# Block 0's weighted sums of gathered expert rows: from VectorE to 32-column TensorE matmuls, two tokens a step

## The chip, the core and the metric

The kernel runs on one core of a Trainium2 chip. The metric is the device time of one execution in microseconds (us), as the median of several runs. A core has a matmul engine (TensorE, PE in the rows; its weight loads are PEld), a vector engine (VectorE, DVE), an activation engine (ScalarE, ACT), a general engine (GpSimd, POOL) and a sync engine that issues DMA transfers (SyncE, SP); the DMA engines move the data. Each engine executes its own instruction stream in order; semaphores tie the streams together.

## The reference, cut to what matters

The program is one decoder layer for 1024 tokens of width 1024: a first norm, one wide projection, two kinds of attention, gates, an output projection, an attention over 256 memory tokens, and last an expert mixer (PEER) of 16,384 experts. The change touches the mixer only:

```
q  = (h @ w_q).reshape(n, 8, 2, 64)                 # 8 heads, two halves
sc = einsum('nhcd,hckd->nhck', q, sub_keys)         # 128 keys in each half
s_top, i_top = top_k(sc, 16)                        # 16 best keys in each half
cand_s = s_top[:, :, 0, :, None] + s_top[:, :, 1, None, :]
cand_i = i_top[:, :, 0, :, None] * 128 + i_top[:, :, 1, None, :]
best_s, pos = top_k(cand_s, 16)                     # 16 best pairs in each head
g = softmax(best_s); idx = cand_i at pos            # 8 x 16 = 128 slots a token
a = einsum('cd,ced->ce', h, u[idx])                 # h . u of each slot's expert
a = gelu(a) * g
out = einsum('ce,ced->cd', a, v[idx])               # weighted sum of 128 rows of v
```

## The kernel before

The 1024 tokens are eight blocks of 128. Everything up to the mixer runs in two token groups of four blocks: projections (P), attentions (T), branch and gate products (G), output projection (O), memory attention (M), expert queries (R). `queries` of the first group are ready when the second group begins, and the mixer of its four blocks (0 to 3) is laid beside the second group's stages.

The mixer is computed in two ways. For blocks 0 to 3 the rows of `u` and `v` are *gathered*: for each of a token's 128 slots one indirect DMA on GpSimd brings 128 rows (one per token, 512 KB) into one of seven row buffers (`R_BUFS`). `gathered_u` multiplies a row by `h3` and sums along it (VectorE, L1039); `gathered_v` adds weight times row to a running sum (L1058). The lane "experts" runs U and V of the blocks in the order of `ORDER`. For blocks 4 to 7 the mixer is *dense*: all 128 groups of 128 experts are multiplied for all 512 tokens, `uT` against `fT` and the result, weighted by a matrix `c`, against `v`. The weights matrix `Wd` is built from the selected slots by `weights` and passes through DRAM. Of the 128 groups (called experts in what follows) the first 48 (`EARLY`) have their `u` product computed first, while `weights` still runs: each one's gelu goes to DRAM (`ga`) and comes back later as `c`. Then all 128 run in turn with two accumulators, `kept` and `out`.

Matmuls of the dense part are three-pass: an operand is split into a high part (ScalarE, L106) and a remainder (VectorE, L107), and `mm3` issues three matmuls (L129 to L131). For the second group's projections, branch and memory products the operands are whole float32 instead (one matmul, L127). The gate products of a group are deferred: `fill` issues them (128 matmuls, four column blocks) beside other work. Transposes go through TensorE into PSUM tiles of the name `tps`, two buffers (`tps()`), from which each consumer copies out. In the second group this holds for keys (L371), queries (L355), attention rows.

Routing (`route`, with `top16` at L928 to L932) finds the top 16 per half and the top 16 pairs, on VectorE, one yield after another; for blocks 0 to 3 in the lane "routes", for 4 to 7 within `weights`.

The order of the work: the program's code emits a main line of stages; at its steps `Pace.tick(us)` gives each lane a budget, and a lane emits its next piece when its price (`U_EACH`, `ROUTE_EACH`) is covered. A scheduler then places every instruction by data dependences and priority; a lane's pieces carry a lag (`ROUTE_LAG`, `EXPERT_LAG`), which puts them behind the main line where both could go. `issue_after` ties an instruction behind another on the same engine. The order within each engine is fixed when the program is built.

## Time and profile before

| | before |
|---|---|
| median of 3 runs | 3502.35 us |
| lowest, highest | 3493.39, 3512.26 us |
| the profiled execution | 3509.34 us |
| its span in the profile | 3507.6 us |
| mean granted TensorE clock in it | 0.928 |

The span is what the instruction records cover; the time of an execution includes a little around it. Busy time of an engine is the sum over its records; matmuls overlap, so TensorE's busy time is above what their starts take. [...] In order of time, the second group's projections take 660 to 1004 us, its attentions end at 1287, branch to queries at 1638; the first 48 experts go to 2119, the first `kept` matmul is at 2240, and the last one ends at 3470.6.

### The profile page before, as it was taken

The numbers are of one execution on the slowest core, as the hardware profiler recorded it, in microseconds if no ns is written. First come the engines' busy times: TensorE is split into PE (matmuls) and PEld (weight loads), VectorE is DVE, ScalarE is ACT, GpSimd is POOL, SyncE is SP. The second block draws the span as 40 slices with busy tenths as digits, with TensorE's granted clock in tenths as the row PEclk, the third lists the DMA queues.
The fourth block names the chain that finished last, engine by engine and source line by source line (L and its number), as shares of the span: only waits on it lengthen the run. The fifth ranks groups of instructions, "written<-read, shape, count | busy, mean of one in ns | idle before, by whom it ended". The sixth has DMA issues, their size and how long they took to land.

```text
span 3507.6 us, 42342 instructions
## 1 busy us (share of the span) xinstructions
PE 3015.4 (86%) x13234; PEld 2285.7 (65%) x13234; DVE 2878.4 (82%) x6695; ACT 1396.7 (40%) x2537; POOL 1380.4 (39%) x1122
## 2 busy tenths in 40 slices
PE   8999888798787698686989995588899999999995
PEld 7777766553355575455767774466687788777884
DVE  6656544599888879888988988687799999999998
ACT  5755344245565441322546456222222222222221
POOL 0000000011235246553131466333466665767665
PEclk9999998999898799888999998799899999999998
DMA  4575443436789579897485899999999999999997
GB/s 138 162 186 133 162 140 137 132 121 198 223 259 312 139 272 356 306 328 272 163 314 189 309 379 341 375 309 321 318 351 372 376 380 365 382 379 373 383 382 265
DMA packets 394210, 964.65 MB, mean 275 GB/s; under 512 B 36712, under 2 KB 146048, under 8 KB 392576
## 3 DMA queue, kind: packets, MB, share of 16 engines
q0 software_dynamic: 155264, 560.01, 45.0%
q1 hardware_dynamic: 238720, 401.94, 33.3%
q8 instruction: 104, 1.70, 0.2%
q14 instruction: 122, 1.00, 0.1%
HBM read 871.64 MB, written 90.18 MB: 274 GB/s over the span
## 4 chain that ended last, share of the span: by engine, by line
PE 35%; DVE 21%; DMA 17%; issue 15%; POOL 8%; ACT 4%; SPq 1%; POOLq 0%; ACTq 0%; DVEq 0%
POOL rows L1036 5%; PE acc L129 5%; PE acc L131 5%; PE acc L130 5%; DMA c<-ga 4%; DVE h3s L1058 3%; DMA rows<-in_peer_v_dram,ii 2%; DMA so<-pq 2%; PE fill L127 2%; POOL rows L1052 2%; PE po L720 2%; DVE rows L1039 2%; DMA fraw<-in_w_in_dram 1%; DMA rows<-in_peer_u_dram,ii 1%; PE tps L601 1%
## 5 line engine op out<-in xcount | busy, mean ns | idle before, releaser
L1036 POOL DMA_INDIRECT rows<-in_peer_u_dram,ii x512 | 656.8, 1283 | 917.2 <-DVE rows L1039 304.9
L1052 POOL DMA_INDIRECT rows<-in_peer_v_dram,ii x512 | 660.6, 1290 | 447.4 <-DVE h3s L1058 290.9
L1058 DVE SCALAR_TENSOR_TENSOR h3s<-rows,wexp,h3s 128x1024 f32<-128x1024 f32 x508 | 651.1, 1282 | 34.4 <-DMA rows<-in_peer_v_dram,ii 25.1
L1039 DVE SCALAR_TENSOR_TENSOR rows<-rows,h3s 128x1024 f32<-128x1024 f32 x512 | 612.0, 1220 | 62.7 <-DMA rows<-in_peer_u_dram,ii 62.2
L129 PE MATMUL acc<-fT,uT 128*128 128x512 f32 x1024 | 415.6, 406 | 38.6 <-ACT uT L106 23.2
L131 PE MATMUL acc<-fT,uT 128*128 128x512 f32 x1024 | 411.8, 402 | 15.3 <-DVE uT L107 15.2
L130 PE MATMUL acc<-fT,uT 128*128 128x512 f32 x1024 | 410.5, 401 | 0.0
L106 ACT ACTIVATE c<-wl 128x512 fp32r<-128x512 f32 x128 | 80.2, 631 | 805.6 <-PE out L130 479.2
L143 POOL TENSOR_TENSOR rstd<-msq,mhalf 128x1 f32<-128x1 f32 (+1 forms) x42 | 34.0, 808 | 596.1 <-DVE msq L141 572.5
L129 PEld LDWEIGHTS acc<-fT,uT 128*128 128x128 f32 x1024 | 196.5, 192 | 84.7 <-ACT uT L106 23.6
L131 PEld LDWEIGHTS acc<-fT,uT 128*128 128x128 f32 x1024 | 196.7, 192 | 64.4 <-DVE uT L107 23.7
L106 ACT ACTIVATE uT<-uraw 128x1024 fp32r<-128x1024 f32 x128 | 135.6, 1059 | 254.2 <-PE acc L130 131.0
L130 PE MATMUL kept<-v,c 128*128 128x512 f32 x512 | 206.2, 405 | 32.3 <-DVE v L107 32.2
L129 PE MATMUL kept<-v,c 128*128 128x512 f32 x512 | 201.4, 400 | 37.1 <-ACT v L106 35.8
L130 PEld LDWEIGHTS acc<-fT,uT 128*128 128x128 f32 x1024 | 197.0, 192 | 45.3 <-issue 6.0
L129 PE MATMUL out<-v,c 128*128 128x512 f32 x512 | 203.6, 398 | 15.2 <-DVE accu L1282 15.2
L107 DVE TENSOR_TENSOR w<-wraw,w 128x512 fp32r<-128x512 f32 (+1 forms) x176 | 116.4, 680 | 116.3 <-ACT w L106 109.5
L131 PE MATMUL kept<-v,c 128*128 128x512 f32 x512 | 203.7, 398 | 0.0
L130 PE MATMUL out<-v,c 128*128 128x512 f32 x512 | 201.9, 394 | 0.0
L131 PE MATMUL out<-v,c 128*128 128x512 f32 x512 | 201.8, 394 | 0.0
L562 ACT ACTIVATE junk<-W,xb 128x384 bf16<-128x384 f32 (+5 forms) x186 | 163.7, 880 | 78.8 <-DVE xb L560 76.1
L127 PE MATMUL acc<-wraw,hT 128*128 128x512 f32 (+1 forms) x384 | 169.3, 597 | 16.2 <-ACT tok L349 7.6
(367 smaller groups left out, 6731.6 us busy)
## 6 DMA issues: line engine op xcount, KB each, us to landing
uraw<-in_peer_ut_dram SPq DMA_DIRECT2D x128, 512.0 KB, 9.2
vraw<-in_peer_v_dram SPq DMA_DIRECT2D x128, 512.0 KB, 8.8
Wd<-wbuf SPq DMA_DIRECT2D x64, 512.0 KB, 8.6
wl<-Wd SPq DMA_DIRECT2D x64, 512.0 KB, 8.4
wraw<-in_w_in_dram SPq DMA_DIRECT2D x40, 512.0 KB, 3.6
fraw<-in_w_in_dram SPq DMA_DIRECT2D x32, 512.0 KB, 6.0
wraw<-in_w_out_dram SPq DMA_DIRECT2D x24, 512.0 KB, 4.2
ga<-gelu SPq DMA_DIRECT2D x48, 256.0 KB, 5.4
```

What stands on the lines that cost most here:

```text
L106: self.nc.scalar.activation(hi, src, AF.Copy)
L107: self.last_dve = self.nc.vector.tensor_tensor(lo, src, hi.bitcast(F32), op=OP.subtract).ins
L127: self.last_pe = nc.tensor.matmul(out, l[0], r[0], start=start, stop=stop).ins
L129: nc.tensor.matmul(out, l[0], r[0], start=start, stop=False)
L130: nc.tensor.matmul(out, l[0], r[1], start=False, stop=False)
L131: self.last_pe = nc.tensor.matmul(out, l[1], r[0], start=False, stop=stop).ins
L562: nc.scalar.activation(junk[:, :(b + 1) * P], self.W[b], AF.Sign, bias=xb[:, j:j + 1].bitcast(F32), accum_out=s[:, j:j + 1])
L720: nc.tensor.matmul(po[:, h * 64:(h + 1) * 64], pT[:, j * P:(j + 1) * P], self.dsv[:, k0 + j, gg * 64:(gg + 1) * 64], start=(k0 + j == 0), ...
L1036: nc.gpsimd.indirect_dma_start(out=u, out_offset=None, in_=a["peer_u"][0], in_offset=bass.IndirectOffsetOnAxis(ap=ii[:, j:j + 1], axis=0))
L1039: nc.vector.scalar_tensor_tensor(u, u, 1.0, h3, op0=OP.mult, op1=OP.mult, accum_out=aa[:, j:j + 1])
L1052: nc.gpsimd.indirect_dma_start(out=v, out_offset=None, in_=a["peer_v"][0], in_offset=bass.IndirectOffsetOnAxis(ap=r["ii"][:, j:j + 1], axi ...
L1058: nc.vector.scalar_tensor_tensor(o, v, w[:, j:j + 1], o, op0=OP.mult, op1=OP.add)
```

## The change

Block 0's V leaves the lane "experts" (`ORDER`), and a lane of its own, "tiled", does it (`tiled_v`). `slots` transposes block 0's slot ids on TensorE (through `tps()`) to `iiT`, where a column holds one token's 128 slots. In each of 64 steps two gathers fetch the 128 rows of `v` of two tokens, and four matmuls of 32 columns contract over the 128 slots: two tokens by two halves of the 1024 columns, each into its own 32 partitions of one PSUM bank (`vacc`). The stationary operand `z` is a 128 x 32 tile of zeros in which the token's own column holds its weights; the 32 tokens of a tile accumulate one after another. A finished PSUM tile goes through ScalarE and DRAM to the block's sum. A step waits for both gathers (`add_manual_dep`) and is tied behind the last emitted matmul; matmuls that `mm3` emits afterwards are tied behind the step (`behind`). The lane starts once the last attention stage has given back its PSUM and block 0's U products are emitted, and it is drained at the end of the first 48 experts. The PSUM bank comes from the stages that follow: five accumulators in G to R for six, three in the first 48 experts for four. SBUF comes from `gelu` and `gT`, one buffer each for two. The price of a gathered item in the last stage is 2.4 for 2.0.

```diff
@@ -80,6 +81,8 @@
     def __init__(self, tc, a, out, dbg=None):
         self.tc, self.nc, self.a, self.out, self.dbg = tc, tc.nc, a, out, dbg
         self.pace = Pace(tc)
+        self.vps = self.pe_gate = None
+        self.multiplied = set()
@@ -121,12 +124,18 @@
+    def behind(self, start=True):
+        return self.tc.issue_after(self.pe_gate) if start and self.pe_gate is not None else nullcontext()
     def mm3(self, out, l, r, start, stop):
         nc = self.nc
         if len(l) == 1:
-            self.last_pe = nc.tensor.matmul(out, l[0], r[0], start=start, stop=stop).ins
+            with self.behind(start):
+                self.last_pe = nc.tensor.matmul(out, l[0], r[0], start=start, stop=stop).ins
             return
-        nc.tensor.matmul(out, l[0], r[0], start=start, stop=False)
+        with self.behind(start):
+            nc.tensor.matmul(out, l[0], r[0], start=start, stop=False)
         nc.tensor.matmul(out, l[0], r[1], start=False, stop=False)
         self.last_pe = nc.tensor.matmul(out, l[1], r[0], start=False, stop=stop).ins
@@ -1023,6 +1032,12 @@
         nc.vector.tensor_copy(r["gg"], r["g"].rearrange("p h s -> p (h s)"))
         r["ii"] = ep.tile([P, P], I32, name="ii", bufs=NG)
         nc.vector.tensor_copy(r["ii"], ids)
+        if b in TILED:
+            t = self.tps()
+            nc.tensor.transpose(t[:, :P], ids, self.ident)
+            r["iiT"] = ep.tile([P, P], I32, name="iiT", bufs=len(TILED))
+            nc.vector.tensor_copy(r["iiT"], t[:, :P])
         yield
@@ -1038,6 +1053,71 @@
             with self.tc.issue_after(self.last_dve):
                 nc.vector.scalar_tensor_tensor(u, u, 1.0, h3, op0=OP.mult, op1=OP.mult, accum_out=aa[:, j:j + 1])
             yield self.u_each
+        self.multiplied.add(b)
+    def tiled_v(self, blks):
+        nc, a, ep = self.nc, self.a, self.ep
+        for b in blks:
+            while self.vps is None or b not in self.multiplied:
+                yield 5.0
+            r = self.rs[b]
+            w = ep.tile([P, P], F32, name="wexp", bufs=1)
+            nc.scalar.activation(w, r["aa"], AF.Gelu)
+            nc.vector.tensor_tensor(w, w, r["gg"], op=OP.mult)
+            o = self.vps.tile([P, 512], F32, name="vacc", bufs=1)
+            nc.tensor.transpose(o[:, :P], w, self.ident)
+            wT = r["gg"].rearrange("p (h s t) -> p h s t", h=2, s=2)
+            nc.scalar.activation(r["gg"], o[:, :P], AF.Copy)
+            done = self.scratch([P, D], f"vo{b}")
+            def gather(n):
+                vs = []
+                for s in range(2):
+                    at = n // 32 * 64 + 32 * s + n % 32
+                    v = self.rows()
+                    i = nc.gpsimd.indirect_dma_start(out=v, out_offset=None, in_=a["peer_v"][0],
+                                                     in_offset=bass.IndirectOffsetOnAxis(ap=r["iiT"][:, at:at + 1], axis=0))
+                    vs.append((v, i.ins))
+                return vs
+            nx = gather(0)
+            for n in range(64):
+                h, t = divmod(n, 32)
+                if t == 0:
+                    o = self.vps.tile([P, 512], F32, name="vacc", bufs=1)
+                if t % 4 == 0:
+                    z = ep.tile([P, 2, 128], F32, name="z", bufs=2)
+                    nc.gpsimd.memset(z, 0.0)
+                    nc.vector.tensor_copy(z[:, :, t:t + 33 * 3 + 1:33], wT[:, h, :, t:t + 4])
+                vs, nx = nx, gather(n + 1) if n < 63 else None
+                with self.tc.high_priority(offset=EXPERT_LAG), self.tc.issue_after(self.last_pe):
+                    m = None
+                    for s in range(2):
+                        for c in range(2):
+                            q = 32 * (2 * s + c)
+                            i = nc.tensor.matmul(o[q:q + 32], z[:, s, 32 * (t % 4):32 * (t % 4) + 32],
+                                                 vs[s][0][:, c * 512:(c + 1) * 512], start=t == 0, stop=t == 31).ins
+                            if m is None:
+                                self.tc.add_manual_dep(i, vs[1][1].name, SYNC, reason="the tokens go together")
+                            m = i
+                self.last_pe = self.pe_gate = m
+                yield self.v_each
+                if t == 31:
+                    e = self.rows()
+                    nc.scalar.activation(e[:, :512], o, AF.Copy)
+                    for s in range(2):
+                        for c in range(2):
+                            q, at = 32 * (2 * s + c), 64 * h + 32 * s
+                            nc.sync.dma_start(done[at:at + 32, c * 512:(c + 1) * 512], e[q:q + 32, :512])
+            self.pe_gate = None
+            o = self.rows()
+            nc.sync.dma_start(o, done)
+            self.finish(b, o, [self.rows() for _ in range(3)])
+            yield 1.0
     def gathered_v(self, b, r):
@@ -1133,7 +1213,7 @@
             nc.tensor.transpose(t[:, P:2 * P], r["g"].rearrange("p h s -> p (h s)"), self.ident)
             ni = wb.tile([P, P], I32, name="ni")
             nc.vector.tensor_copy(ni, t[:, :P])
-            gT = wb.tile([P, P], F32, name="gT", bufs=2)
+            gT = wb.tile([P, P], F32, name="gT", bufs=1)
             nc.scalar.activation(gT, t[:, P:2 * P], AF.Copy)
             yield 1.0
@@ -1188,7 +1268,7 @@
             stores.pop(0)()
             yield 3.0
-    def dense(self, psum, early):
+    def dense(self, psum, early, vpx):
         nc, a = self.nc, self.a
@@ -1221,11 +1301,13 @@
                 self.pace.add("weights", self.weights(blks))
                 for e in range(early):
                     o = first(e)
-                    t = self.wb.tile([P, 512], F32, name="gelu", bufs=2)
+                    t = self.wb.tile([P, 512], F32, name="gelu", bufs=1)
                     nc.scalar.activation(t, o, AF.Gelu)
                     ga[e] = self.scratch([P, 512], f"ga{e}")
                     nc.sync.dma_start(ga[e], t)
                 self.pace.drain("weights")
+                self.pace.drain("tiled")
+                vpx.close()
             self.route_ctx.close()
             psum = self.psum_phase(psum, "ps3", A_BUFS)
             kept = {}
@@ -1333,8 +1415,11 @@
-            psum = self.psum_phase(psum, f"psG{g}", 6)
             last = g == len(GROUPS) - 1
+            if last:
+                vpx = ExitStack()
+                self.vps = vpx.enter_context(self.pool("vps", side="right", space=PSUM))
+            psum = self.psum_phase(psum, f"psG{g}", 5 if last else 6)
@@ -1375,18 +1460,21 @@
                 self.u_each = U_EACH[0]
                 self.pace.add("routes", routes, ROUTE_EACH, ROUTE_LAG)
                 self.pace.add("experts", self.experts(routes), None, EXPERT_LAG)
+                self.v_each = V_TILED
+                self.pace.add("tiled", self.tiled_v(TILED), None, EXPERT_LAG)
         self.pace.drain("routes")
         psum = self.psum_phase(psum, "ps2", D_BUFS)
-        psum = self.dense(psum, EARLY)
+        psum = self.dense(psum, EARLY, vpx)
 EARLY = 48
 V_AHEAD, V_EACH = 0, None
-ORDER = [("U", 0), ("V", 0), ("U", 1), ("V", 1), ("U", 2), ("V", 2), ("U", 3), ("V", 3)]
+TILED, V_TILED = (0,), 6.0
+ORDER = [("U", 0), ("U", 1), ("V", 1), ("U", 2), ("V", 2), ("U", 3), ("V", 3)]
-H_BUFS, D_BUFS, R_BUFS = (4, 2), 4, 7
+H_BUFS, D_BUFS, R_BUFS = (4, 2), 3, 7
@@ -1394,7 +1482,7 @@
-U_EACH, ROUTE_EACH = (1.9, 1.8, 1.9, 1.3, 2.0), 3.0
+U_EACH, ROUTE_EACH = (1.9, 1.8, 1.9, 1.3, 2.4), 3.0
```

The order on TensorE at the end of the second group's projections, before: the gate products (`fill`), the projections (`acc<-wraw,hT`) and the transposes of keys (`k_...`) and queries (`tok`).

```order
L127 MATMUL fill<-hT_6126,fraw 128x512 x2
L127 MATMUL acc<-wraw,hT_6126 128x328 x8
L127 MATMUL fill<-hT_6126,fraw 128x512
L371 MATMUL tps<-ident,k_6655 128x128 x3
L127 MATMUL acc<-wraw,hT_6126 128x512
L371 MATMUL tps<-ident,k_6680 128x128 x2
L127 MATMUL acc<-wraw,hT_6126 128x512
```

The same place after, with the transpose of the slot ids (`ids`):

```order
L135 MATMUL fill<-hT_6126,fraw 128x512 x2
L135 MATMUL acc<-wraw,hT_6126 128x328 x8
L135 MATMUL fill<-hT_6126,fraw 128x512
L135 MATMUL acc<-wraw,hT_6126 128x512 x32
L135 MATMUL fill<-hT_6126,fraw 128x512 x125
L1038 MATMUL tps<-ident,ids 128x128
L380 MATMUL tps<-ident,k_6659 128x128 x3
L380 MATMUL tps<-ident,k_6684 128x128 x3
```

All 32 remaining projection matmuls and all 125 remaining gate products now stand in front of the first key transpose, and the transpose of the ids stands between.

The order on VectorE in the first of the dense experts, before: the remainder splits `uT` of experts 4 to 6 (the numbers are buffers) and routing instructions, the rows between them left out.

```order
L107 TENSOR_TENSOR uT_14007<-uraw,uT_14006 128x1024
L975 MAX key<-ci 128x8
...
L996 TENSOR_REDUCE ids<-eq 128x32
L107 TENSOR_TENSOR uT_14108<-uraw,uT_14107 128x1024
...
L932 MAX_INDEX i_15117<-v_15116,t_15120 128x8
L107 TENSOR_TENSOR uT_14176<-uraw,uT_14175 128x1024
```

The same place after, experts 4 to 8:

```order
L110 TENSOR_TENSOR uT_14369<-uraw,uT_14368 128x1024
...
L1251 SCALAR_TENSOR_TENSOR ah<-dot,gT 128x512
L110 TENSOR_TENSOR uT_14481<-uraw,uT_14480 128x1024
...
L110 TENSOR_TENSOR uT_14557<-uraw,uT_14556 128x1024
...
L1138 SCALAR_TENSOR_TENSOR h3s<-rows,wexp,h3s 128x1024
L110 TENSOR_TENSOR uT_14620<-uraw,uT_14619 128x1024
L1138 SCALAR_TENSOR_TENSOR h3s<-rows,wexp,h3s 128x1024 x2
L110 TENSOR_TENSOR uT_14733<-uraw,uT_14732 128x1024
```

Between the splits of experts 4 and 5 stood 20 VectorE instructions and now stand 291; 98 more come before that of expert 6 and 211 before that of expert 7, after which two stand before the next.

The order on TensorE in the branch products of the second group, before:

```order
L127 MATMUL acc<-oT_8649,wraw 128x512 x64
```

The same place after, with the matmuls of the steps (`vacc`):

```order
L135 MATMUL acc<-oT_8653,wraw 128x512 x13
L1101 MATMUL vacc<-rows,z 32x512
L135 MATMUL acc<-oT_8653,wraw 128x512 x2
L1101 MATMUL vacc<-rows,z 32x512
L135 MATMUL acc<-oT_8653,wraw 128x512
L1101 MATMUL vacc<-rows,z 32x512 x10
L135 MATMUL acc<-oT_8653,wraw 128x512 x10
```

The 64 branch matmuls, which stood together, have matmuls of steps between them, often one at a time. Over the whole program the 256 matmuls of the 64 steps stand in 119 runs, 73 of them of a single matmul and 36 of four; 38 steps lie in the stages G to R, 26 in the first 48 experts, the last of these before expert 33.

## Rows read from the trace of the kernel before

**Rows 1.** The page of the profile: busy time, share, instructions; one DMA group.
```profile
span 3507.6 us, 42342 instructions
...
PE 3015.4 (86%) x13234; PEld 2285.7 (65%) x13234; DVE 2878.4 (82%) x6695; ACT 1396.7 (40%) x2537; POOL 1380.4 (39%) x1122
...
ga<-gelu SPq DMA_DIRECT2D x48, 256.0 KB, 5.4
```
**Rows 2.** Windows by stage: us; busy PE, PEld, DVE, ACT, POOL; PEclk; DMA; GB/s.
```profile
728.00:1004.00 276.00, 225.57 (x641) 113.63 (x641) 243.38 (x1161) 164.16 (x329) 50.32 (x49) 0.91 0.60 189
...
1287.00:1638.00 351.00, 266.27 (x886) 173.67 (x886) 304.78 (x495) 81.11 (x157) 208.96 (x171) 0.84 0.90 334
...
1679.00:2013.00 334.00, 301.66 (x1533) 234.58 (x1532) 300.84 (x1131) 178.19 (x230) 94.32 (x73) 0.96 0.68 248
...
2119.00:2240.00 121.00, 65.19 (x384) 51.29 (x384) 97.54 (x110) 58.90 (x75) 74.04 (x58) 0.81 0.95 355
2240.00:2594.00 354.00, 303.74 (x1212) 239.68 (x1213) 285.97 (x386) 85.78 (x113) 142.52 (x115) 0.92 0.93 321
2594.00:3452.00 858.00, 839.42 (x3652) 687.56 (x3651) 821.05 (x991) 235.69 (x306) 568.36 (x424) 0.99 1.00 375
```
**Rows 3.** Timeline of PE in the last experts: start us, us, engine, line.
```profile
3439.72 0.39 PE L130 MATMUL out<-v,c 128*128 128x512 f32 x1
...
3441.08 0.39 PE L130 MATMUL out<-v,c 128*128 128x512 f32 x1
```
**Rows 4.** Instruction groups by line: count, busy us, mean ns, idle before and its releaser.
```profile
L1058 DVE SCALAR_TENSOR_TENSOR h3s<-rows,wexp,h3s 128x1024 f32<-128x1024 f32 x508 | 651.1, 1282 | 34.4 <-DMA rows<-in_peer_v_dram,ii 25.1
L1039 DVE SCALAR_TENSOR_TENSOR rows<-rows,h3s 128x1024 f32<-128x1024 f32 x512 | 612.0, 1220 | 62.7 <-DMA rows<-in_peer_u_dram,ii 62.2
...
L1171 DVE SCALAR_TENSOR_TENSOR ah<-dot,gT 128x512 f32<-128x512 f32 x128 | 87.9, 687 | 12.0 <-PE dot L1165 9.7 <-PE out L1175 0.6
...
L1144 DVE TENSOR_SCALAR bi<-ni 128x128 int32<-128x128 int32 x56 | 8.7, 236 | 0.3 <-PE out L1152 0.3
...
L1177 ACT ACTIVATE wbuf<-out 128x512 f32<-128x512 f32 x128 | 134.1, 1078 | 21.4 <-PE out L1175 21.2
L1169 ACT ACTIVATE oh<-dot,m 128x512 f32<-128x512 f32 x128 | 87.1, 683 | 55.6 <-PE out L1175 44.1 <-PE dot L1165 11.1
```
**Rows 5.** Timeline of PE at the end of the second group's projections.
```profile
698.31 0.67 PE L371 MATMUL tps<-ident,k 128*128 128x128 f32 x3 [1.77 <-DVE tok L322]
...
705.62 22.48 PE L127 MATMUL acc<-wraw,hT 128*128 128x512 f32 x52
```
**Rows 6.** Windows, gate products (fill) alone: PE, PEld, ACT busy; PEclk; DMA; GB/s.
```profile
728.00:1004.00 276.00, 66.70 (x129) 25.01 (x130) 5.27 (x8) 0.91 0.60 189
1004.00:1287.00 283.00, 60.47 (x123) 22.63 (x121) 5.46 (x8) 0.87 0.75 236
```
**Rows 7.** Instruction groups of the routing on VectorE.
```profile
L932 DVE FIND_INDEX8 i<-v,t 128x8 uint32<-128x128 f32 x128 | 36.2, 285 | 0.0
L928 DVE MAX8 v<-so 128x8 f32<-128x128 f32 x128 | 33.7, 282 | 55.5 <-DMA so<-pq 55.5
...
L993 DVE TENSOR_TENSOR eq<-kp,fpos 128x512 f32<-128x512 f32 x32 | 21.8, 681 | 0.0
...
L932 DVE FIND_INDEX8 pos<-best,t 128x8 uint32<-128x50 f32 x64 | 12.9, 204 | 0.0
```
**Rows 8.** Timeline of VectorE: remainder splits of experts 4 and 7.
```profile
1661.46 1.21 DVE L107 TENSOR_TENSOR uT<-uraw,uT 128x1024 fp32r<-128x1024 f32 x1
...
1678.84 1.21 DVE L107 TENSOR_TENSOR uT<-uraw,uT 128x1024 fp32r<-128x1024 f32 x1
```
**Rows 9.** Timeline of one late expert: its stored product loaded and used.
```profile
2248.05 0.33 SPq L1249 DMA_DIRECT2D c<-ga  x1
...
2253.63 0.69 DVE L1253 TENSOR_TENSOR wl<-c,wl 128x512 f32<-128x512 f32 x1 [1.35 <-DMA c<-ga]
```
**Rows 10.** Timeline of the end: the last matmul.
```profile
3470.17 0.39 PE L131 MATMUL out<-v,c 128*128 128x512 f32 x1
```

More of the change, by code (lines that the diff above doesn't have):

```diff
@@ L1 @@
 import math
-from contextlib import ExitStack
+from contextlib import ExitStack, nullcontext
 import concourse.bass as bass
@@ L30 @@
 EPS = 1e-6
+SYNC = mybir.DependencyInfo(mybir.DependencyClass.Sync, mybir.DependencyReason.DATA)
 NEG = -1.0e30
```

## The prediction, made before the changed kernel was run

> **What bounds the kernel now.** I read the page first: a span of 3507.6 us with TensorE busy 86% and VectorE 82% [rows 1]. Both are high, so no share says which one counts, and I cut the span into stages [rows 2]. In the second half of the projections of the second token group (728 to 1004 us) VectorE is busy 243 of 276 us; in the branch, memory and query stage (1287 to 1638) 305 of 351 with the DMA engines at 0.90; in the early experts (1679 to 2013) 301 of 334; in the late ones (2594 to 3452) 821 of 858, with the DMA at 1.00 and TensorE at 839. So VectorE carries the middle of the program, and at the end three engines are full together. TensorE's share there is of records that overlap: successive 512-column matmuls start 0.227 us apart though each record is 0.39 us long [rows 3], so the 3652 matmuls of the last stretch are 828 us of work.
>
> The profiled execution took 3509.3 us, 1.7 us round its span; the median of the runs is 3502.35. I add to the first and take 7 us off at the end.
>
> **What is removed.** Block 0's 128 sums of gathered rows leave VectorE: 128 x 1.28 = 164 us [rows 4]. As many gathers stay, one per token in place of one per slot, so DMA bytes do not change.
>
> **What is added on TensorE.** 64 steps of four matmuls of 32 columns on float32 rows. No row shows a 32-column matmul. The nearest is a float32 matmul on the whole array: 52 records in 22.48 us, two records to a matmul, 0.86 us each [rows 5]. A step is then 0.86 us (all four together) to 3.44 us (one after the other); 55 to 220 us in all. Below nothing it can't be. I take 3.44 in the branch stage, where the new order puts most of the four apart between whole-array matmuls, and leave both ends open in the dense stage, where they stand together.
>
> [...] In the new order 119 runs of such matmuls stand between others, 73 of them single. [...]
>
> **Where the time comes from: two stretches of the new order.** Durations are rows of before, counts are of the instruction orders.
>
> *Projections.* The added transpose of block 0's slot ids takes a buffer of the two that the projection's own transposes rotate through, and its place on TensorE is behind all 128 gate matmuls ("fill"). Before, three of these stood ahead of the key transposes, and the other 125 ran beside projections and attention, 129 and 123 records in the two stretches [rows 6]. Now 125 x 0.86 = 107 us stand between the last projection matmul (705.62 + 22.48 = 728.1 us) and the key transposes, which began at 698.3 [rows 5]; they can't start before about 838. VectorE fills the pause with routing: 326 search instructions, 2.7 blocks' worth, are moved ahead. A block's searches cost 5 rows of some 35 us over 8 blocks = 22 us, the three rows like L993 8 us, the five 50-wide ones about 8 [rows 7]: 38 us, 103 us in all. That work is not lost. But VectorE then waits some 30 us and still has its 243 us of 728 to 1004 [rows 2], less 103, plus 54 more gathered products at 1.22 (66 us), plus some 20 that stood between the first key transposes' users and 728 (my choice, at that stretch's 0.88): 226 us. 838 + 226 = 1064 against 1004: +60. Attention (1004 to 1287) gives back some: 19 sums (24 us) and 53 us of TensorE's gate work (123 records by 0.43) are gone from it; I take -20. Net **+40** (0 to +70).
>
> *Branch to queries, 1287 to 1638.* VectorE has 103 gathered items in place of 146, 55 us less. But 38 steps bring 76 gathers. 334 GB/s x 351 us = 117 MB; minus 43 and plus 76 half-megabyte gathers is 134 MB, at the 375 GB/s of the full stretch [rows 2] 359 us. TensorE takes up to 38 x 3.44 = 131 us more, in a stage where it was busy 266 of 351 by overlapping records. **+10** (-10 to +50).
>
> *Early experts.* Before, the lo splits uT of experts 4 to 7 stood at 1661.5 (the 4th) and 1678.8 us (the 7th) [rows 8]: 17 us. In the new order 358 searches and 239 other routing instructions (3 blocks, 114 us by the 38 above), 70 instructions of the weights lane (0.24 to 0.69 us by L1144 and L1171 [rows 4], I take 0.4: 28) and 25 gathered sums (32) stand between experts 4 and 7: 174 us, less a little overlap; I take 167, so +150. TensorE has in that time three experts' chains (24 x 0.227 = 5.4 us each), one weights block and a few steps: it starves. Why that is a loss though the routing must be done anyway: VectorE's relief afterwards (experts 7 to 40: 115 gathered by 1.27, 33 splits by 1.22 and some 38 us of weights make 224 us, before 301) can't be used. The gathers of that stretch rise by 41 items and 42 rows: 248 GB/s x 334 = 83 MB, plus 43, minus about 5 of stores: 121 MB, 324 us at 375 GB/s; TensorE needs 32 x 5.4 + 50 of weights + 19 to 75 of steps = 242 to 298. So the DMA bounds it: -10. The stretch from the 48th expert to the first "kept" matmul, 2119 to 2240, had VectorE busy 98 us [rows 2], 45 x 1.28 = 58 of it gathered sums ahead of the last weights block; those are fewer now and ScalarE's pace for the block, 32 x (0.68 + 1.08) = 56 us [rows 4], takes over: I choose -25. Net **+115** (+50 to +150).
>
> *Late experts.* 413 gathered items are left in place of 554, and the pace is one per 2.4 in place of 2.0. VectorE loses 141 x 1.25 = 176 us there. TensorE does not: 858 - 828 = 30 us of idle, of which I take -20. From 2240 to 2594 items stay nearly the same, and each expert still waits for its stored product (5.6 us from issue to use, then 0.69 [rows 9]), 48 x 6.3 = 300 of 354: -5. After the last matmul (3470.2 + 0.4 [rows 10]) the span runs on for 37 us, through the last gathered sums and the stores behind them; the order has six sums fewer there, 6 x 1.28 = 8, and I add half as much for the queues: -12. Together **-37** (-15 to -60).
>
> Single buffers (gelu, gT) and one accumulator fewer I cost at nothing: an early expert takes 334 / 33 = 10 us, a store of the gelu buffer 5.4 [rows 1]; the cover is the rest of those 10, and without it the price is up to 48 x 5.4 = 259 us. I keep 0 to 50 in the range. The 16 cleared z tiles are short work for a POOL that is busy 39% [rows 1].
>
> **Sum**: 40 + 10 + 115 - 37 = +128; 3509.3 + 128 - 7 = 3630 us.
>
> **Rivals.**
> - *VectorE's total is what counts* (faster). The moved routing has to be done in any case, and VectorE's work falls by some 160 us. If it lost no time at the two places, it would spend 17 us ahead of the late experts on 13 more finished items (483 in place of 470), and gain the 37 there and the 20 of the attention: 3502 + 17 - 37 - 20 = 3462. For it: VectorE is the fullest engine from 660 to 2119. Against: it is served in order, and between experts 4 and 7 TensorE has nothing else. 0.18.
> - *The steps cost TensorE what they can* (slower still). One after the other plus waits for gathers: seven row buffers now serve two users, a step holds four, and POOL, whose queue is in order, stands before a gather until a step has released its rows. 64 x 3.44 = 220 us, of which my sum holds some 130 at most under other work; from experts 7 on TensorE's 298 and the waits would add 60 to 110: 3715. For it: no pause of TensorE is free from 1679 to 2013. [...] 0.12.
> - *No change*: half of the early terms come true, the rest is covered. 3502 + 40 + 10 - 37 is about 3510. 0.08.
> - My forecast has 0.62.
>
> Its own range is 3565 to 3700. To hold 8 in 10 the range reaches down past "no change" and up to the second rival: 3480 to 3710; some 0.16 lies below, 0.04 above. What a measurement tells from no change is 0.5%, 17 us. Slower: 0.62 + 0.12 = 0.74; same 0.08; faster 0.18.
>
> **What will show it.** Right: key transposes of the second group at about 840 us in place of 698, and all gate matmuls ahead of them; a gap of 150 us or more between the uT splits of experts 4 and 7 with TensorE mostly idle; the first "kept" matmul some 165 us later than 2240; after that a late stretch with TensorE full and VectorE near 0.85. Wrong: if the first "kept" matmul comes before 2260, the moved routing was free and the first rival holds; if the steps' records start 0.86 us apart and experts 7 to 40 take over 380 us, the second.

## The result, and the profile after

The changed kernel took 3867.60 us (median of 4 runs, 3865.31 to 3870.33), the kernel before 3503.47 beside it: a ratio of 1.1029, interval [1.1006, 1.1051]. The forecast was 3630 us, in a range of 3480 to 3710. The direction was right, the size was not: 364 us in place of 128. Ratios here and below leave out the few executions in a slower state (two of ten of `before_room`, one of ten of `before_no_sums`).

The page of the profile after, busy time by engine:

```profile
span 3867.0 us, 43205 instructions
...
PE 3212.9 (83%) x13748; PEld 2333.0 (60%) x13748; DVE 2749.3 (71%) x6584; ACT 1393.1 (36%) x2538; POOL 1331.0 (34%) x1138
```

Against [rows 1], VectorE has 129 us less to do and TensorE 198 us more. The stretches that answer to [rows 2], with the same columns:

```profile
728.00:853.00 125.00, 112.73 (x250) 47.57 (x249) 94.52 (x661) 10.60 (x17) 9.54 (x8) 0.96 0.51 162
853.00:1142.00 289.00, 194.57 (x553) 101.44 (x551) 240.92 (x665) 172.42 (x348) 128.23 (x106) 0.82 0.73 252
1142.00:1424.00 282.00, 190.07 (x1129) 164.05 (x1129) 227.13 (x657) 156.57 (x417) 108.46 (x94) 0.78 0.64 193
1424.00:1512.00 88.00, 83.51 (x212) 27.23 (x212) 41.30 (x68) 5.58 (x9) 38.95 (x38) 0.97 0.79 280
1512.00:1856.00 344.00, 281.40 (x960) 150.69 (x960) 194.12 (x408) 76.51 (x148) 162.94 (x156) 0.91 0.80 279
...
1882.00:2088.00 206.00, 98.11 (x498) 67.53 (x499) 192.31 (x966) 65.41 (x90) 37.42 (x31) 0.71 0.31 96
2088.00:2442.00 354.00, 279.48 (x1336) 204.71 (x1335) 222.82 (x275) 115.01 (x151) 199.47 (x170) 0.89 0.98 375
...
2655.00:3010.60 355.60, 307.50 (x1219) 243.46 (x1220) 281.29 (x336) 84.64 (x111) 136.47 (x109) 0.92 0.90 305
3010.60:3838.90 828.30, 827.47 (x3646) 683.71 (x3645) 687.40 (x821) 237.88 (x307) 385.00 (x300) 1.00 0.87 313
```

Read them in order. A new stretch of 125 us (728 to 853) holds gate products on TensorE. Projections and attentions then take about as long as before (289 us for 276, and 282 for 283). Branch to queries (1424 to 1856) is longer, with TensorE busy 365 of 432 us and VectorE only 235. A pause of 206 us (1882 to 2088) has VectorE busy and TensorE not. The last row is TensorE's own time for its matmuls, 827 of 828 us.

The two places of the order, in the trace. TensorE, answering to [rows 5]:

```profile
699.72 26.85 PE L135 MATMUL acc<-wraw,hT 128*128 128x512 f32 x62 [0.56 <-DVE r L330]
726.40 11.32 PE L135 MATMUL fill<-hT,fraw 128*128 128x512 f32 x26
...
814.99 37.94 PE L135 MATMUL fill<-hT,fraw 128*128 128x512 f32 x80 [5.42 <-DMA fraw<-in_w_in_dram]
852.77 0.27 PE L1038 MATMUL tps<-ident,ids 128*128 128x128 f32 x1
852.88 0.49 PE L380 MATMUL tps<-ident,k 128*128 128x128 f32 x3
```

The key transposes come at 852.9 us in place of 698.3. VectorE, answering to [rows 8], the remainder splits of experts 4, 5 and 7:

```profile
1882.24 1.21 DVE L110 TENSOR_TENSOR uT<-uraw,uT 128x1024 fp32r<-128x1024 f32 x1
...
1992.94 1.22 DVE L110 TENSOR_TENSOR uT<-uraw,uT 128x1024 fp32r<-128x1024 f32 x1
...
2087.43 1.22 DVE L110 TENSOR_TENSOR uT<-uraw,uT 128x1024 fp32r<-128x1024 f32 x1
```

From expert 4 to 7 it is 205 us in place of 17. What TensorE waited for from 1882 to 2092 (total, times, longest, us):

```profile
PE vacc L1101 <- DVE z L1094: 59.2, 1, 59.2
PE out L1212 <- DVE ids L1005: 20.7, 2, 15.6
PE vacc L1101 <- DMA rows<-in_peer_v_dram,iiT: 11.3, 2, 10.0
```

The longest gap of the pause is not among these waits, since TensorE works on matmuls of the weights meanwhile. Expert 2's last matmul starts at 1878.6 us and expert 3's first at 1984.7, behind a step whose gather GpSimd began only at 1978.2, after it had waited 53 us, the last of them for routing on VectorE (L940):

```profile
1978.18 1.23 POOL L1080 DMA_INDIRECT rows<-in_peer_v_dram,iiT  x1 [52.99 <-DVE v L940]
1982.85 1.94 PE L1101 MATMUL vacc<-rows,z 128*32 128x512 f32 x8 [1.30 <-DMA rows<-in_peer_v_dram,iiT]
1984.72 0.80 PE L138 MATMUL acc<-fT,uT 128*128 128x512 f32 x1
```

And the steps themselves, first in the branch products (two records to a 32-column matmul):

```profile
1499.02 1.04 PE L1101 MATMUL vacc<-rows,z 128*32 128x512 f32 x2
1499.99 1.12 PE L135 MATMUL acc<-oT,wraw 128*128 128x512 f32 x2
1501.05 1.04 PE L1101 MATMUL vacc<-rows,z 128*32 128x512 f32 x2
```

Then in the early experts, all four matmuls of a step in one row of eight records:

```profile
2346.82 1.06 PE L1101 MATMUL vacc<-rows,z 128*32 128x512 f32 x8 [2.22 <-issue]
2347.82 0.50 PE L138 MATMUL acc<-fT,uT 128*128 128x512 f32 x1
```

One matmul alone holds TensorE for 0.97 us before the next starts, four together for 1.00 (the granted clock is 1.00 in both places).

Where the time went, from marks in the traces: the end of the attentions (T end), the remainder splits of experts 0, 8 and 48 (e0, e8, e48), the first and last split of `v` (v0, v127), and the end of the span. The first column is a time, the others are steps in us; the last are the gathers begun by e0 and e48.

| kernel | median | T end | to e0 | to e8 | to e48 | to v0 | to v127 | to end | gathers |
|---|---|---|---|---|---|---|---|---|---|
| before | 3503 | 1286 | 352 | 47 | 430 | 125 | 1212 | 55 | 299, 419 |
| after | 3868 | 1424 | 432 | 236 | 455 | 108 | 1184 | 28 | 368, 614 |
| ids_late | 3803 | 1285 | 504 | 234 | 456 | 111 | 1183 | 28 | 367, 613 |
| no_gate | 3756 | 1424 | 436 | 51 | 465 | 136 | 1213 | 28 | 368, 525 |
| ids_late_no_gate | 3571 | 1288 | 396 | 62 | 478 | 126 | 1201 | 28 | 333, 498 |
| both_no_matmuls | 3563 | 1281 | 373 | 45 | 459 | 129 | 1243 | 28 | 329, 485 |
| both_no_wait | 3582 | 1281 | 403 | 46 | 490 | 132 | 1200 | 28 | 347, 515 |
| both_two_ahead | 3600 | 1289 | 409 | 48 | 481 | 131 | 1202 | 28 | 341, 499 |
| both_as_many_gathers | 3689 | 1283 | 407 | 58 | 468 | 105 | 1231 | 145 | 304, 420 |
| one_matmul_a_step | 3615 | 1285 | 378 | 47 | 436 | 105 | 1222 | 144 | 307, 420 |
| as_many_no_matmuls | 3567 | 1280 | 350 | 48 | 417 | 103 | 1219 | 142 | 308, 420 |
| both_half_pace | 3676 | 1287 | 391 | 53 | 465 | 171 | 1223 | 79 | 296, 419 |

So the 360 us between the two spans are 137 by the end of the attentions, 80 to expert 0, 189 to expert 8, 25 to expert 48, -17 to v0, -28 to v127 and -27 behind it.

### The profile page after: what moved, and what is told of

Its sections match the earlier page's. It is cut to its first block, busy times and chain, and to the rows that moved or that the text cites. A ratio compares the mean times of both kernels' runs of the same rounds, so it can differ in the third digit from the quotient of the medians.

```text
span 3867.0 us, 43205 instructions
## 1 busy us (share of the span) xinstructions
PE 3212.9 (83%) x13748; PEld 2333.0 (60%) x13748; DVE 2749.3 (71%) x6584; ACT 1393.1 (36%) x2538; POOL 1331.0 (34%) x1138
## 5 line engine op out<-in xcount | busy, mean ns | idle before, releaser
L1051 POOL DMA_INDIRECT rows<-in_peer_u_dram,ii x512 | 643.3, 1256 | 862.3 <-DVE rows L1054 488.6
L1132 POOL DMA_INDIRECT rows<-in_peer_v_dram,ii x384 | 470.5, 1225 | 552.1 <-DVE h3s L1138 334.5
L1138 DVE SCALAR_TENSOR_TENSOR h3s<-rows,wexp,h3s 128x1024 f32<-128x1024 f32 x381 | 488.3, 1282 | 87.9 <-DMA rows<-in_peer_v_dram,ii 78.3
L138 PE MATMUL acc<-fT,uT 128*128 128x512 f32 x1024 | 409.8, 400 | 0.5 <-DVE wl L1335 0.5
L140 PE MATMUL acc<-fT,uT 128*128 128x512 f32 x1024 | 404.2, 395 | 4.5 <-DVE uT L110 4.5
L139 PE MATMUL acc<-fT,uT 128*128 128x512 f32 x1024 | 404.1, 395 | 0.0
L1080 POOL DMA_INDIRECT rows<-in_peer_v_dram,iiT x128 | 150.6, 1177 | 260.9 <-PE vacc L1101 106.3
L1101 PE MATMUL vacc<-rows,z 128*32 128x512 f32 x512 | 135.6, 660 | 111.2 <-DVE z L1094 61.7
```

Source lines behind the costliest of these rows:

```text
L138: nc.tensor.matmul(out, l[0], r[0], start=start, stop=False)
L139: nc.tensor.matmul(out, l[0], r[1], start=False, stop=False)
L140: self.last_pe = nc.tensor.matmul(out, l[1], r[0], start=False, stop=stop).ins
L1051: nc.gpsimd.indirect_dma_start(out=u, out_offset=None, in_=a["peer_u"][0], in_offset=bass.IndirectOffsetOnAxis(ap=ii[:, j:j + 1], axis=0))
L1080: i = nc.gpsimd.indirect_dma_start(out=v, out_offset=None, in_=a["peer_v"][0], in_offset=bass.IndirectOffsetOnAxis(ap=r["iiT"][:, at:at + ...
L1101: i = nc.tensor.matmul(o[q:q + 32], z[:, s, 32 * (t % 4):32 * (t % 4) + 32], vs[s][0][:, c * 512:(c + 1) * 512], start=t == 0, stop=t == 3 ...
```

## The experiments

**The two places in the order.** `ids_late` takes the transpose of the ids out of `slots` and makes it in `tiled_v`:

```diff
-            t = self.tps()
-            nc.tensor.transpose(t[:, :P], ids, self.ident)
 ...
+            nc.vector.tensor_copy(w, r["ii"])
+            o = self.vps.tile([P, 512], F32, name="vacc", bufs=1)
+            nc.tensor.transpose(o[:, :P], w, self.ident)
```

> The changed kernel, with the transpose of block 0's slot ids moved from the routing (where it takes one of the two tps buffers in front of the second group's key transposes) into the start of tiled_v, on the vacc bank. Theory (the two places in the order are stalls of their own): the 125 gate products no longer stand in front of the key transposes, these run near 700 us in place of 853, and the 137 us that the second group's attentions ended late are gone: 3867 - 137 = 3730 us. Rival 1 (VectorE's total counts; what was moved ahead only comes later): the routing goes back behind the transposes and the gain is at most 40 us: 3830 to 3867. Rival 2 (the steps' own cost is the loss): nothing changes, 3867.

`no_gate` empties the tie:

```diff
-        return self.tc.issue_after(self.pe_gate) if start and self.pe_gate is not None else nullcontext()
+        return nullcontext()
```

> The changed kernel without the tie of mm3's first matmuls behind the last step (behind() does nothing); steps stay tied behind the main line. Theory: the pile of 291, 98 and 211 VectorE instructions between the uT splits of experts 4, 5, 6 and 7 comes from that tie: expert 5's first matmul stands behind a step whose z copy is on VectorE behind low-priority routing. Without it the splits of experts 4 and 8 are again about 24 us apart in place of 210, and the time is 3867 - 185 = 3680 us. Rival 1 (VectorE's total): the routing is done later and costs the same there: 3830 to 3867. Rival 2 (steps' own cost): 3867 or more, since the steps now come later.

> Both of the above together. Theory: the two add up: 3867 - 137 - 185 = 3545 us, that is 40 us above before, which is the 81 us of branch to queries and some 20 of the later early experts, less 55 at the end. Rival 1 (VectorE's total, so that only its relief counts once the order is mended): VectorE has 160 us less to do, 3350 to 3480. Rival 2 (the steps' own cost): above 3700.

Measured: 3802.90 us (1.0842 [1.0808, 1.0876]), 3756.26 (1.0710 [1.0670, 1.0751]) and both 3570.65 (1.0165 [1.0131, 1.0200]). Each edit removed its place entirely: T end is at 1285 us, and the splits of experts 4 and 8 stand 23 us apart. But alone each gave some 70 us back: `ids_late` 72 of its 137 from T end to expert 0, `no_gate` 67 of its 185 behind expert 8. Together they give 297, near the theory's 322. In `ids_late` what came back is a wait of the tied order, TensorE's largest from 1285 to 1430 us:

```profile
PE vacc L1101 <- DMA rows<-in_peer_v_dram,iiT: 65.5, 4, 58.9
```

With the tie in place a step that waits for its gather holds the branch matmuls behind it. In `no_gate` what came back is later: 525 gathers are begun by expert 48 in place of 614, and the stretches behind it are 58 us longer. There rival 1 holds in part: the pause had done work. One likely reason why the two edits together give more than their sum is in the order: the steps stand in 62 runs there and hold TensorE for 79 us, in `ids_late` in 103 runs and 126 us, in `no_gate` in 126 runs and 145 us.

**The room.** Before, with five and three accumulators and single `gelu` and `gT`:

```diff
-H_BUFS, D_BUFS, R_BUFS = (4, 2), 4, 7
+H_BUFS, D_BUFS, R_BUFS = (4, 2), 3, 7
```

> The kernel before, with only the room taken away that the change takes: five accumulators for six in the second group's branch to queries, three for four in the first 48 experts, one gelu and one gT buffer for two. My prediction cost these at nothing: 3503, within 0.5%. Rival: the smaller room is part of the 81 us lost from branch to queries and of the slower early experts: 3530 to 3600.

3521.52 us, 1.0035 [1.0013, 1.0057]: some 12 us, all of it from expert 32 to v0. Within the bound that I had called no change, but not nothing.

**What the remaining 64 us are.** From `ids_late_no_gate`: without most step matmuls, with a resident tile in place of the gathered rows, and with gathers two steps ahead.

```diff
-                    for s in range(2):
+                    for s in range(2 if t in (0, 31) else 0):
```

> ids_late_no_gate with 240 of the 256 step matmuls left out (only the first and last step of each PSUM tile keep theirs); all gathers stay. Leaves out most of block 0's sums. Theory (the 64 us that are left over before are TensorE's: 64 steps of about 1.05 us are 67, and it waits 68 us for step gathers, part of it under other work): both go, 3571 - 67 - 40 = 3465 us, the early experts again near 477 us from e0 to e48. Rival (the gathers themselves, moved into a stretch in which the DMA is full, cost the time): above 3540.

```diff
-                                                 vs[s][0][:, c * 512:(c + 1) * 512], start=t == 0, stop=t == 31).ins
+                                                 self.ident[:, None, :].to_broadcast([P, 4, P]), start=t == 0, stop=t == 31).ins
```

> ids_late_no_gate with the step matmuls reading a resident tile in place of the gathered rows: TensorE does the same matmuls and waits for no gather; the gathers are still issued. The sums of block 0 are then not those of the rows. Theory: TensorE's waits go and its 67 us of steps stay: 3571 - 40 = 3530 us. Rival A (the steps' time is the whole loss): 3571. Rival B (the waits are the whole loss): 3500 or less.

```diff
-            nx = gather(0)
+            nx = [gather(0), gather(1)]
```

> ids_late_no_gate with the gathers of a step issued two steps ahead in place of one. Theory: TensorE's 68 us of waits for step gathers shrink to some 20: 3540 us. Rival (seven row buffers, of which the steps then hold up to six: the other gathers wait): 3575 or more.

3562.86 us (1.0154), 3582.07 (1.0212) and 3599.53 (1.0275). All three theories missed in the total. The stretches say more: without the matmuls T end to expert 48 is 877 us for 936, so 59 us go with the steps, but one of the steps that stay waits 32 us for its gather behind expert 48, and the late part is 42 us longer. The 48 us that stay above the 829 of before come with 66 more gathers begun. On this way the steps had held TensorE for 68 us, of which 5 stay:

```profile
1288.00:1684.00 396.00, 35.40 (x240) 5.33 (x240) 0.00 (x0) 0.00 (x0) 0.86 0.92 338
1684.00:2224.00 540.00, 32.92 (x208) 4.76 (x208) 0.00 (x0) 0.60 (x1) 0.94 0.78 286
```

These are the rows of `vacc` in `ids_late_no_gate`, with busy PE, PEld, DVE and ACT. Without waits more gathers begin (515 by expert 48) and nothing is won (939 us). Two steps ahead is slower in the median, as its rival said; its stretches are those of `ids_late_no_gate` within 14 us, so the rival's reason is not shown.

**What VectorE's relief is worth.**

```diff
+                    if b == 0 and j > 0:
+                        pass
-                    if j == 0:
+                    elif j == 0:
```

> The kernel before with 127 of block 0's 128 sums left out and nothing in their place; all gathers stay. It shows what VectorE's relief is worth by itself (block 0's output is then that of one slot). My rival 1 (VectorE's total counts) would have 127 x 1.28 = 163 us less: 3340. My forecast's late gain only (TensorE's 30 us of idle in the late experts, and a shorter tail): 3507 - 57 = 3450. No gain at all: 3500.

3513.25 us, 1.0019 [1.0003, 1.0035]: nothing, as long as the prices of the lanes stay. Of block 0's sums 122 of 127 stood in branch to queries, so this stage alone is tested. Branch to queries with 127 sums fewer, the columns of [rows 2]:

```profile
1287.00:1638.00 351.00, 264.46 (x891) 171.28 (x891) 158.27 (x379) 81.28 (x157) 166.13 (x162) 0.85 0.86 324
```

VectorE is busy 158 us there in place of 305, and the stretch ends at the same time.

**As many gathers as before.** Prices of items raised so that items and step gathers together stand as before, then the same without most step matmuls, and steps at half the pace:

```diff
+                self.u_each = 5.0
-U_EACH, ROUTE_EACH = (1.9, 1.8, 1.9, 1.3, 2.4), 3.0
+U_EACH, ROUTE_EACH = (1.9, 1.8, 1.9, 4.0, 2.0), 3.0
```

> ids_late_no_gate with the prices of gathered items raised from the branch stage to the 48th expert (1.9 and 1.3 to 5.0 and 4.0) and set back to 2.0 behind it, so that items and step gathers together stand as they did before (297 by expert 0 and 411 by expert 47 in the order; before 292 and 408; ids_late_no_gate 328 and 491). Theory: the 64 us left are the 75 gathers more that the new lane pulls into stretches in which the DMA is full (75 x 0.52 MB at 375 GB/s = 105 us), given back only in part later; without them 3507 to 3535 us. Rival (the steps themselves, 64 x 1.05 us on TensorE, are the loss): 3570 or more, since 613 gathered items are then left for the late experts.

> both_as_many_gathers with 240 of the 256 step matmuls left out (most of block 0's sums are then missing); all gathers stay. With as many gathers as before and almost no step on TensorE nothing of either cause is left. Theory: within 15 us of before, 3495 to 3525, and the difference to both_as_many_gathers is what the steps cost TensorE (0 to 67 us). Rival (something else, the room or the order): above 3540.

```diff
+                self.u_each = 3.0
-TILED, V_TILED = (0,), 6.0
+TILED, V_TILED = (0,), 12.0
-U_EACH, ROUTE_EACH = (1.9, 1.8, 1.9, 1.3, 2.4), 3.0
+U_EACH, ROUTE_EACH = (1.9, 1.8, 1.9, 3.0, 2.0), 3.0
```

> ids_late_no_gate with as many gathers again (289 by expert 0, 408 by expert 47), but shared otherwise: steps at half the pace (price 12 for 6; 19 of 64 by expert 0, 38 by expert 47, the other 26 drained behind the 48 experts), items at price 3.0. Theory (gathers count): as both_as_many_gathers up to expert 47, then the drain of 26 steps adds 52 gathers in a row, 52 x 1.4 = 73 us less what the drain of the weights covers: 3530 to 3590. Rival (the steps' cost on TensorE while it is full counts): fewer steps beside full TensorE, so faster than both_as_many_gathers.

3689.07 us (1.0519), 3567.00 (1.0175) and 3675.52 (1.0491). All three theories missed in the total, since the totals carry 79 to 145 us behind the last split of `v`, where items held back at the dearer price are left over (78 of them behind the last matmul in the first two, 30 in the third); the question is answered by T end to expert 48. With the steps it is 933 us, at 420 gathers; without them 815; before, 829 at 419. At equal gathers the steps cost 118 us, so my theory that the gathers are the loss fell for this order. But it is another order: the same edit left the steps in 123 runs in place of 62, and they hold TensorE for 135 us in place of 79. The step matmuls alone (TensorE busy first, matmuls side by side counted once), first with all of them:

```profile
1283.00:1690.00 407.00, 77.18 (x296) 10.74 (x296) 0.00 (x0) 0.60 (x1) 0.91 0.83 295
1690.00:2217.00 527.00, 58.19 (x216) 8.10 (x216) 0.00 (x0) 0.59 (x1) 0.97 0.69 244
```

The same with most left out:

```profile
1280.00:1630.00 350.00, 10.30 (x24) 1.33 (x24) 0.00 (x0) 0.60 (x1) 0.86 0.92 343
1630.00:2095.00 465.00, 1.06 (x8) 0.16 (x8) 0.00 (x0) 0.59 (x1) 0.97 0.78 275
```

135 us of TensorE against 11: a difference of 124, and 118 lost. At half the pace, 39 steps by expert 48 hold TensorE for 85 us, and it is 909 us: faster up to there, as the rival said, and given back behind it (171 us to v0). Gathers ahead are not free either: with the matmuls left out in both, 485 gathers by expert 48 make 877 us and 420 make 815, 0.95 us for each gathered item, its sum on VectorE included.

**By run, by matmul or by gather.**

```diff
+                            if s + c < 2 and t not in (0, 31):
+                                continue
```

> both_as_many_gathers with one matmul in each step in place of four (all four in the first and last step of a PSUM tile, so that 76 of 256 stay, in 66 runs of adjacent step matmuls in place of 123); all gathers stay, most of block 0's sums are missing. From the end of the attentions to expert 48 it took 933 us with 256 matmuls and 815 with 16. Theory (a run of step matmuls costs TensorE about 1.1 us whether it holds one or four): 815 + (66 - 10) x 1.1 = 877 us. Rival A (each matmul costs by itself, 118 us for 240): 815 + 60 x 0.49 = 845. Rival B (a step costs by the gathers it makes TensorE wait for): about 930.

T end to expert 48 took 861 us, between the 877 by runs and the 845 by matmuls. The steps' own time on TensorE:

```profile
1285.00:1662.00 377.00, 48.54 (x92) 6.13 (x92) 0.00 (x0) 0.60 (x1) 0.89 0.88 318
1662.00:2145.00 483.00, 29.74 (x60) 4.15 (x60) 0.00 (x0) 0.59 (x1) 0.98 0.74 267
```

78 us for 76 matmuls in 66 runs (1.19 a run), against 135 for 256 in 123 (1.10 a run, 0.53 a matmul). Engine time went by runs where a run held about one step or less: 1.10 to 1.27 us a run in the six orders of 62 to 126 runs that are counted here and above (136 us for 119 runs in the changed kernel, 1.14). Where steps stand together, as in `both_no_wait` with 64 steps in 25 runs, it is 71 us, 1.11 a step. Of the engine time two thirds (45 of 67 us) showed up in the stretch. Leaving matmuls out also takes away waits for gathers (from 1283 to 2217 us TensorE waits 23.4 us for step gathers in `both_as_many_gathers`, and less than 6.0 in `as_many_no_matmuls`). It may free row buffers sooner: GpSimd waited 139.5 us for step matmuls in `ids_late_no_gate`, and no run shows how much of that goes with them. Only `both_no_wait`, which keeps the matmuls alone, bears on that: 939 us against the 877 of `both_no_matmuls`, 62 more for 66 us more of steps on TensorE, but with 30 more gathers begun, which at 0.95 each would be 28 of the 62 (an estimate).

**The other edits.** The last stage's price back at 2.0 in the changed kernel; the kernel before with 1.8 there; and with lower prices earlier:

```diff
-U_EACH, ROUTE_EACH = (1.9, 1.8, 1.9, 1.3, 2.4), 3.0
+U_EACH, ROUTE_EACH = (1.9, 1.8, 1.9, 1.3, 2.0), 3.0
```

> The changed kernel with the price of a gathered item in the last stage at 2.0 again in place of 2.4. I had put the change of price into the late gain without a sum of its own. Theory (413 items are left and TensorE is full from there on, 828 us for 3652 matmuls): the same, 3867 within 0.5%. Rival (VectorE at 0.83 then hinders it again): 3880 to 3895.

> The kernel before with the price of a gathered item in the last stage at 1.8 in place of 2.0, nothing else: the items end before the last matmul. Theory (27 us of the late 55 us that the changed kernel gained are the shorter tail, which can be had without it): 3480 to 3490. Rival (VectorE is then what holds the late experts): 3505 or more.

```diff
-U_EACH, ROUTE_EACH = (1.9, 1.8, 1.9, 1.3, 2.0), 3.0
+U_EACH, ROUTE_EACH = (1.4, 1.3, 1.4, 1.3, 2.0), 3.0
```

> The kernel before with lower prices of gathered items in the second group's projections and attentions (1.8 and 1.9 to 1.3 and 1.4): 363 items by expert 0 and 472 by expert 47 in the order in place of 292 and 408, so as many gathers ahead as in ids_late_no_gate, with no step, and pulled into stages in which the DMA is at 0.60 and 0.75. Theory (where the DMA is not full a gather ahead is free, and late it gives TensorE's 30 us of idle and the tail of 27 back): 3450 to 3480. Rival (VectorE is what bounds those stages): 70 x 1.25 = 88 us more there, 3540.

3882.79 us (1.1080 [1.1062, 1.1097]): the price is worth 15 us, as the rival said. What TensorE waits for most in the last stretch, before, with the price back at 2.0, and after (total, times, longest, us):

```profile
PE acc L129 <- DVE wl L1253: 15.4, 10, 3.4
PE acc L138 <- DVE wl L1335: 11.4, 6, 3.1
PE acc L138 <- DVE wl L1335: 0.5, 1, 0.5
```

The 15 us are of the pace and not of the amount of work: VectorE is busy 690 us at the price of 2.0 and 687 at 2.4, but by quarters of the stretch 200, 199, 210 and 81 for 193, 174, 176 and 145. 3514.15 (1.0021 [1.0012, 1.0030]): not the theory's gain; the tail, which the lower price was to take away, stayed at 56 us. 3572.43 (1.0195 [1.0167, 1.0223]): the 71 items more did not go into projections and attentions (T end stays at 1284 us, 141 gathers by then) but between them and the memory stage's norm; TensorE's largest wait from 1410 to 1640 is for that norm:

```profile
PE tps L156 <- DVE h L148: 94.6, 2, 90.2
```

In the 90 us VectorE ran 58 gathered sums (74.5 us) ahead of the end of that norm. No version beat the kernel before.

## Why the prediction was wrong

Against the forecast of 40 + 10 + 115 - 37 = +128 us the stretches gave 137 + 80 + 197 - 55 = +359. Three terms were too small, and in all three what failed is the cover: relief on VectorE that was to be given back, or work that was to lie under other work. Of the signs, the late transposes, the gap between the splits and the full TensorE at the end came; the first `kept` matmul came 415 us later than before (2655 us), not 165.

*The first step failed where it was tested.* "VectorE carries the middle of the program" was read from its busy share. `before_no_sums` shows that 147 us of that work can go from branch to queries and the stretch stays at 351: there it was filler, paced in by a price, and bounded nothing. For projections and early experts no run shows as much by itself.

*Projections, +40 forecast, 137 measured.* The stall and its cause were right: the transposes stand behind 125 gate products, at 853 for the forecast 838 (from 726 to 853 the gate products waited 8.8 us for loads and 3.4 for ScalarE's copies), and `ids_late` takes it away to the microsecond. Wrong was what I gave back: 103 us of routing moved ahead and 20 us in the attentions. I had made VectorE's work, 226 us, the length of what follows the transposes; it took 289 us, with VectorE busy 241 of them. The transposes were 154 us late, and 20 came back on the way to the first attention masks (253 us for 273); the attentions then gave nothing. The 60 us of gate products [rows 6] were gone from them, but the stage took 282 us for 283, with TensorE's granted clock at 0.78 for 0.87. Whether the clock took back what the missing work gave, no run shows.

*Branch to queries, +10 forecast, 80 measured.* I set the steps' upper bound at 131 us and let them lie beside other work, and worked the term out from DMA bytes. The steps stand in 91 runs there and hold TensorE for 99 us, and its busy time rose from 266 to 365 us while VectorE's fell from 305 to 235. The later orders bear out that TensorE's time counts here: with and without the steps, at equal gathers, the stretch to expert 0 is 407 and 350 us, for 77 and 10 us of steps. The bound was right, the cover was not there. The forecast left a step between 0.86 and 3.44 us; measured are 1.00 us for four matmuls together and 0.97 for one alone, so a step cut into four single matmuls is 3.88 us by my estimate from the second. A single matmul and the whole-array one behind it took 0.97 + 1.06 = 2.03 us, against 1.72 for two whole-array ones [rows 5], all at a granted clock of 1.00: some 0.3 us more. What a change between 32 columns and the whole array costs by itself no run shows.

*Early experts, +115 forecast, 197 measured.* The pause was forecast at +150 and is +189 (experts 0 to 8), and its form is as forecast: VectorE 192 of 206 us busy, TensorE 98. I had not seen its cause, which `no_gate` shows: `behind` ties experts' matmuls to steps that wait for low-priority work. Expert 3 stands 106 us behind a step whose gather came late, expert 5 behind a step whose `z` copy has the lane's low priority on VectorE (59 us in one wait); meanwhile all routing that was ready went first. For experts 8 to 48 I took -10 and got +25: more gathers (209 for 117 in that stretch) and most of the 28 runs of steps that stand in the early experts. The stretch from expert 48 to v0 came nearly as forecast (-17 for -25); the room, costed at nothing, is some 12 us.

*Late, -37 forecast, -55 measured.* The mechanism was right in this: TensorE was busy 827 of the 828 us, and VectorE no longer hinders it (TensorE waits 0.5 us for `wl` in place of 15.4). But the 176 us less work that I named as the reason is half of it: v0 to v127 is 1212 us before, 1198 in `price_as_before`, with the same work on VectorE as after, and 1184 after. The tail is 28 us for 55, where I took -12. The price of 2.4, which I left without a term, is 15 us of the gain.

*The range* ended at 3710 since I let both stretches overlap with relief. With each term at its upper bound (70, 50, 150, -15) my own sum would have reached 3757; only the second rival priced the steps without cover, and it kept the projections at +40.

What stays open: why two thirds and not all of the steps' engine time shows in `one_matmul_a_step`; how much of a step's cost is TensorE's time and how much waits and held row buffers; and how much of what the tie and the ids' place give together beyond their sum (297 us against 65 + 111) is due to the fewer runs.

## What to carry to other kernels

Take an engine for the bound only if taking work from it would move the end: leave the work out once and look, stage by stage. When an added stream is tied in front of or behind the main one on an engine that runs its instructions in the program's order, as TensorE did here (expert 3 stood 106 us behind a step), follow the lowest-priority thing that it waits for (here a copy of 8 elements a partition, and a gather that stood behind others) and price the main stream's wait for it. And price small matmuls by runs, from a row of the trace: here four that stood together took TensorE 1.00 us, and one that the scheduler had set apart 0.97, at a granted clock of 1.00 both times.

## What the runs showed of the hardware

Four 32-column float32 matmuls into four different groups of 32 output partitions took TensorE 1.00 us together, and one alone 0.97, both at a granted clock of 1.00; at 0.50, behind 103 us in which TensorE was busy 63 at 0.81, the four took 1.87 (1982.85 to 1984.72). A gathered item more (512 KB and its sum on VectorE) cost about 0.95 us from `as_many_no_matmuls` (420 gathers, 815 us, the DMA at 0.92 and 0.78 in its two stretches) to `both_no_matmuls` (485, 877). TensorE's granted clock was 0.71 over the pause in which it was busy 98 of 206 us, and 1.00 in the last 828 us, which it filled.
